# Moving the down-projection's weight rows to the split-weight slots, summing in place, and merging the operand stores

## The chip, the cores and the metric

The kernel runs on 1 core of one Trainium2 chip. The metric is the device time of one execution in microseconds (us); lower is better. The core's engines are PE (matrix products; PEld is its weight load), DVE (VectorE, elementwise work), ACT (ScalarE), POOL (GpSimd) and SP (SyncE, which here only issues DMAs). ACT issues DMAs too, from the same in-order instruction stream as its arithmetic.

## The reference, cut to what matters

One decoder block on 1024 tokens of width 1024: retention and sparse attention, merged, then a gated feed-forward part, all in float32. The change lies in the feed-forward part:

```
def conv_ffn(h, w_up, conv_w, conv_b, w_down):
    a, b = jnp.split(h @ w_up, 2, axis=-1)          # w_up: 1024 x 5632
    ac = conv_b + sum(conv_w[i] * a_pad[:, i:i + S] for i in range(CONV_W))
    return (jax.nn.gelu(ac) * b) @ w_down            # w_down: 2816 x 1024
```

## The kernel before, in words

**Products.** Every float32 product is made from three reduced-precision ones: each operand is split into a high and a low part (`split`, lines 129 and 130: ACT copies the high part, DVE subtracts it to get the low part) and `mm3` (lines 133 to 135) issues three matmuls of 128x128 by 128x512. Both feed-forward products are done as 2x2 block products with seven multiplications in place of eight (Winograd's form of Strassen's scheme), so that sums and differences of blocks of both operands have to be made first.

**Up-projection.** `up(f)` handles a pair of 128-column blocks of the hidden width (11 pairs). For each pair, `seven` (line 954) runs twice: once for the half `a` (which then goes through the convolution and GELU in `conv`, line 1002) and once for the half `b` (which multiplies the result, `out_b`, line 1012). Each run makes seven products of 12 matmuls. `up_weights` (line 903) loads two raw weight tiles `wu_raw` (line 908), forms the block sums `t12`, `t34` (lines 914, 915, 932, 933) and splits them: the sums into `wt`, the three plain blocks into `d11`, `d21`, `d22`. The seventh product of each run is put off into the next run (`late`), so `out_b(2)` of a pair (line 1016) runs inside the next pair.

**Operands of the down-projection.** When `out_b(2)` is done, lines 1026 to 1035 form four sums `s1` to `s4` of the gated result into two tiles `gs`, and ACT stores each to DRAM. Between the two runs of `seven`, `down_sums` (line 1037) loads two tiles of rows of `w_down` (`wd_raw`, line 1042), forms four sums into two tiles `ws` (lines 1048 to 1051), and ACT stores each (line 1053). With the three blocks of the gated result stored by line 1023 that is eleven stores per pair.

**Slots.** Tiles with one tag share a fixed number of slots. `wu_raw`, `wd_raw` and later `dn_raw` share three slots of 4 KB per partition (pool `wraw`, tag `raw`). `d11`, `d21`, `d22`, `gs` and `ws` share four slots with the tag `wh` and four with the tag `wl` (pool `wsp`). A load is issued when its slot is free. `rows` holds the gated result of a pair (`ac`) and is written again by the next pair's `conv`.

**Down-projection.** `down` (line 1092) runs over seven operands and 11 pieces each: `piece` (line 1069) loads a tile `dn_raw` with the row operand beside the weight operand, splits it, and 12 matmuls use it. Four of the seven operands come from the scratch `p_scr` (one DMA per piece), three from `g_scr` and `w_down` (two DMAs per piece).

**Order.** Each engine runs its own instructions in a fixed order. The order is chosen when the kernel is built, by a planner that lays the instructions on a simulated time line, takes what is ready, and prefers what stands earlier in the program. It is not written by hand here, and nothing reorders it on the chip: an engine that comes to an instruction whose data is missing waits there.

```
    wraw = ctx.enter_context(tc.tile_pool(name="wraw", bufs=3))
    wsp = ctx.enter_context(tc.tile_pool(name="wsp", bufs=4))
```

Of the kernel before, what the change touches and what calls it, by code (L numbers as in the profile page):

```python
# [10 lines left out]
F32 = mybir.dt.float32  # L11
# [7 lines left out]
P = 128  # L19
# [65 lines left out]
def tile_hybrid_block(ctx: ExitStack, tc: tile.TileContext, x, norm_mix, w_in, ret_gn_g,  # L85
# [4 lines left out]
    nc = tc.nc  # L90
    x, out = x[0], out[0]
# [5 lines left out]
    wraw = ctx.enter_context(tc.tile_pool(name="wraw", bufs=3))  # L97
    wsp = ctx.enter_context(tc.tile_pool(name="wsp", bufs=4))
# [8 lines left out]
    def scratch(name, n, shape):  # L107
        return [dram.tile(list(shape), F32, name=f"{name}{i}") for i in range(n)]
# [19 lines left out]
    def split(hi, lo, src):  # L128
        nc.scalar.activation(hi, src, AF.Copy)  # L129
        nc.vector.tensor_sub(lo, src, f32(hi))  # L130
# [9 lines left out]
    def weights(parts, kt=KD, raw_eng=None):  # L140

        n = sum(q[2] for q in parts)
        raw = wraw.tile([P, kt, n], F32, name="w_raw", tag="raw")
        c = 0
        for src, c0, w in parts:
            nc.sync.dma_start(raw[:, :, c:c + w],
                              src[:kt * P, c0:c0 + w].rearrange("(k p) c -> p k c", p=P))
            c += w
        wh = wsp.tile([P, kt, n], F32R, name="w_hi", tag="wh")
        wl = wsp.tile([P, kt, n], F32R, name="w_lo", tag="wl")  # L150
        split(wh, wl, raw)
        return wh, wl
# [413 lines left out]
    with ExitStack() as st:  # L566
# [32 lines left out]
        for h in range(H_R):  # L599
# [27 lines left out]
            if h < SPILL_Q:  # L627
                raw = wraw.tile([P, S], F32, name="q_raw", tag="raw")
# [28 lines left out]
            if h < SPILL_V:  # L657
                for hf in range(2):
                    raw = wraw.tile([P, 4, DV], F32, name="v_raw", tag="raw")
# [8 lines left out]
            for t in range(NT):  # L668
                hf, j = t // 4, t % 4
                c = slice(j * P, (j + 1) * P)  # L670
                tok = slice(t * P, (t + 1) * P)
                if wp:
                    ps = bank("mm")[:, 0:DV]
                    for k in range(KD):
                        wh, wl = wp[k // 4]
# [7 lines left out]
                if h == H_R - 1 and t == NT - 1:  # L683
# [4 lines left out]
                    for k in range(KD):  # L688
                        n = S if k < KD - 2 else 512
                        raw = wraw.tile([P, S], F32, name="r_raw", tag="raw")  # L690
# [78 lines left out]
    with ExitStack() as st:  # L769
        pool = st.enter_context(tc.tile_pool(name="mtmp", bufs=2))  # L770
        for mi in range(KD):
            wh, wl = weights([(w_ret_o, mi * P, P)])
# [40 lines left out]
    NP = NF // 2  # L813
    g_scr = {i: scratch(f"g_{i}", NP, (P, 512)) for i in ("a11", "a12", "s4")}

    p_scr = {i: scratch(f"p_{i}", NP, (P, 2, 512)) for i in ("s1", "s2", "s3", "a22")}

    def rms_row(t, xr, gain, dst=None):
        hx = fpool.tile([P, D], F32, name="hx", tag="ft", bufs=4)
# [15 lines left out]
    def block_pair(name):  # L835
        return [mpool.tile([P, 4, 512], F32R, name=name + i, tag="B") for i in "hl"]
# [3 lines left out]
    for ch in range(2):  # L840
        cs = slice(ch * 512, ch * 512 + 512)
        for t in (range(NT) if ch == 0 else (4, 5, 6, 7, 0, 1, 2, 3)):
            hf, j = t // 4, t % 4
# [11 lines left out]
            if t == 4:  # L855
                a22, s1 = block_pair("a22"), block_pair("s1")

                fa = big.tile([P, 2, 4, 512], F32, name="fa", tag="A")
            if t == 0:
                a11, a12 = block_pair("a11"), block_pair("a12")  # L860
                s4t = big.tile([P, 2, 4, 512], F32R, name="s4", tag="A")
                s4 = [s4t[:, i] for i in range(2)]
# [25 lines left out]
    s2, s3 = block_pair("s2"), block_pair("s3")  # L888
# [65 lines left out]
    def seven(c0, out):  # L954

        (t1, t2, t3, t4), (b11, b21, b22) = up_weights(c0)

        m = fpool.tile([P, 2, 512], F32, name="m", tag="ft", bufs=4)

        def kept(ps, i):  # L960
            nc.scalar.activation(m[:, i], ps, AF.Copy)
            return m[:, i]

        c = bank("sc")
        product(c, s1, t1, True, True)
        m5 = kept(c, 0)
        xb = bank("mm")
        product(xb, a11, b11, True, True)
        m1 = kept(xb, 1)
        while late:  # L970
            late.pop()()
        yb = bank("pt")
        product(yb, a12, b21, True, True)
        out(0, yb, m1)
        product(xb, s2, t2, False, True)
        u2 = kept(xb, 1)
        product(c, s4, b22, False, True)
        out(1, c, u2)
        product(xb, s3, t3, False, True)
        out(3, xb, m5)  # L980

        def last():
            product(xb, a22, t4, False, True)
            out(2, xb, None)
        late.append(last)

    def up(f):
        ar, ac = rows[:, 0], rows[:, 1]
        done = []

        def out_a(i, in0, in1):
            dst = ar[:, i % 2, T1 if i >= 2 else T0]
            if in1 is None:
                nc.scalar.activation(dst, in0, AF.Copy)
            else:
                nc.vector.tensor_add(dst, in0, in1)
            done.append(i)
            for e in range(2):
                if i in (e, e + 2) and e in done and e + 2 in done:
                    conv(e)  # L1000

        def conv(e):
            k = f + e
            nc.scalar.activation(ac[:, e], ar[:, e], AF.Identity, scale=cw[:, 2, k:k + 1],  # L1004
                                 bias=cw[:, 3, k:k + 1])
            nc.vector.scalar_tensor_tensor(ac[:, e, 1:S], ar[:, e, 0:S - 1], cw[:, 1, k:k + 1],
                                           ac[:, e, 1:S], op0=OP.mult, op1=OP.add)
            nc.vector.scalar_tensor_tensor(ac[:, e, 2:S], ar[:, e, 0:S - 2], cw[:, 0, k:k + 1],
                                           ac[:, e, 2:S], op0=OP.mult, op1=OP.add)
            nc.scalar.activation(ac[:, e], ac[:, e], AF.Gelu_apprx_tanh)  # L1010

        def out_b(i, in0, in1):
            tok = T1 if i >= 2 else T0
            g = ac[:, i % 2, tok]
            if in1 is None:
                nc.vector.tensor_mul(g, in0, g)
            else:
                nc.vector.tensor_add(in1, in0, in1)
                nc.vector.tensor_mul(g, in1, g)
            n = f // 2  # L1020
            if i != 2:
                dst = g_scr[("a11", "a12")[i]][n] if i < 2 else p_scr["a22"][n][:, 0, :]
                nc.scalar.dma_start(dst, g)
                return

            a11, a12, a21, a22 = (ac[:, e, t] for t in (T0, T1) for e in range(2))
            s = [wsp.tile([P, 2, 512], F32, name="gs", tag=t) for t in ("wh", "wl")]
            s1, s2, s3, s4 = (x[:, j] for x in s for j in range(2))
            nc.vector.tensor_add(s1, a21, a22)
            nc.vector.tensor_sub(s2, s1, a11)  # L1030
            nc.vector.tensor_sub(s3, a11, a21)
            nc.vector.tensor_sub(s4, a12, s2)  # L1032
            for name, v in (("s1", s1), ("s2", s2), ("s3", s3)):
                nc.scalar.dma_start(p_scr[name][n][:, 0, :], v)
            nc.scalar.dma_start(g_scr["s4"][n], s4)

        def down_sums():

            raws = []
            for e in range(2):  # L1040
                raw = wraw.tile([P, 2, 512], F32, name="wd_raw", tag="raw")
                nc.sync.dma_start(raw, w_down[(f + e) * P:(f + e + 1) * P, :].rearrange(
                    "p (h c) -> p h c", h=2))
                raws.append(raw)
            b11, b12, b21, b22 = (r[:, h] for r in raws for h in range(2))
            t = [wsp.tile([P, 2, 512], F32, name="ws", tag=t) for t in ("wh", "wl")]
            t1, t2, t3, t4 = (x[:, j] for x in t for j in range(2))
            nc.vector.tensor_sub(t1, b12, b11)
            nc.vector.tensor_sub(t2, b22, t1)
            nc.vector.tensor_sub(t3, b22, b12)  # L1050
            nc.vector.tensor_sub(t4, b21, t2)
            for name, v in (("s1", t1), ("s2", t2), ("s3", t3), ("a22", t4)):
                nc.scalar.dma_start(p_scr[name][f // 2][:, 1, :], v)

        seven(f * P, out_a)
        down_sums()
        seven(DFF + f * P, out_b)

    for f in range(0, NF, 2):
# [8 lines left out]

    def piece(name, n):
        raw = wraw.tile([P, 2, 512], F32, name="dn_raw", tag="raw")  # L1070
        if name in p_scr:
            nc.sync.dma_start(raw, p_scr[name][n])
        else:
            e, h = {"a11": (0, 0), "a12": (1, 0), "s4": (1, 1)}[name]
            r0 = (2 * n + e) * P
            nc.sync.dma_start(raw[:, 0], g_scr[name][n])
            nc.sync.dma_start(raw[:, 1], w_down[r0:r0 + P, h * 512:h * 512 + 512])
        w = mpool.tile([P, 2, 2, 512], F32R, name="dn", tag="B")
        split(w[:, 0], w[:, 1], raw)
        return w  # L1080
# [45 lines left out]
    for t in range(4):  # L1126
        final(t)

    ws = [piece("a22", n) for n in range(NP)]
    for j in range(4):  # L1130
        for n in range(NP):
            part(xb[j], ws[n], j, False, n == NP - 1, True)
        v = x1[4 + j][:, 0:512]
# [24 lines left out]
```

## Time and profile before

| | |
|---|---|
| median of 3 runs | 1798.89 us (1797.86 to 1800.18) |
| profiled execution | 1798.08 us |
| its span, first to last instruction | 1796.3 us |
| outside the span | 1.8 us |
| PE busy | 1722.9 us, 96% of the span |
| DVE busy | 1116.9 us, 62% |
| ACT busy | 802.2 us, 45% |
| mean granted PE clock | 0.987 |
| moved by DMA | 231.56 MB |

The busy share says how long an engine had something in work. PE's matmuls overlap in their pipeline, so that a busy PE need not be at its peak; the spacing of their starts says how fast they go. A wait names what came last for the waiting instruction. A timeline row begins with the start and the duration in us; a bracket at its end gives the idle time before it and what ended that.

### The profile page before, as it was taken

How to read it: one execution, taken by the hardware profiler on the slowest of the kernel's cores; microseconds unless marked ns; L12 is line 12 of the kernel's file. 1: busy time of each engine (PE TensorE's matmuls, PEld its weight loads, DVE VectorE, ACT ScalarE, POOL GpSimd, SP SyncE). 2: the span in 40 equal slices, each digit the busy share in tenths (PEclk: the TensorE clock that was granted, in tenths of full speed). 3: DMA queues.
4: the chain of work that ended last, by engine and by line, in shares of the span. 5: the costliest groups of instructions: out<-in, count | busy, mean ns of one | idle time of the engine just before them, and what ended most of it. 6: DMA issues, size and time to landing. Idle time of an engine off the chain costs nothing.

```text
span 1796.3 us, 24206 instructions
## 1 busy us (share of the span) xinstructions
PE 1722.9 (96%) x9005; PEld 1458.4 (81%) x9005; DVE 1116.9 (62%) x2332; ACT 802.2 (45%) x1425; POOL 86.6 (5%) x94
## 2 busy tenths in 40 slices
PE   7999999999999999999999896999998999999998
PEld 7888898988989998899777785877777777788886
DVE  6637676666766845565535348667667677665654
ACT  5435555455555744444544224433334343334442
POOL 1000000000000001221012000000000000000000
PEclk9999999999999999999999998999999999999999
DMA  6352222222221233222866311334444444487762
GB/s 207 106 144 75 64 67 63 63 74 74 62 71 57 74 118 98 83 86 78 257 216 216 133 71 69 114 135 153 154 150 157 142 143 139 158 296 241 232 209 107
DMA packets 177044, 231.56 MB, mean 129 GB/s; under 512 B 11558, under 2 KB 118558, under 8 KB 176926
## 3 DMA queue, kind: packets, MB, share of 16 engines
q1 hardware_dynamic: 137390, 167.34, 30.4%
q10 hardware_dynamic: 39536, 62.67, 9.4%
q8 instruction: 71, 1.16, 0.3%
q14 instruction: 47, 0.39, 0.1%
HBM read 163.12 MB, written 66.85 MB: 128 GB/s over the span
## 4 chain that ended last, share of the span: by engine, by line
PE 80%; DVE 8%; DMA 7%; ACT 2%; issue 2%; POOL 0%; SPq 0%; DVEq 0%; ACTq 0%; POOLq 0%
PE ps_mm L133 16%; PE ps_mm L134 15%; PE ps_mm L135 15%; PE ps_sc L135 4%; PE ps_sc L133 4%; PE ps_sc L134 4%; PE ps_pt L509 3%; PE ps_pt L135 2%; PE ps_pt L134 2%; PE ps_pt L133 2%; PE ps_sc L396 2%; PE ps_sc L395 2%; PE ps_pv L516 2%; PE ps_pv L515 2%; DMA sga<-ga_scr 1%
## 5 line engine op out<-in xcount | busy, mean ns | idle before, releaser
L133 PE MATMUL ps_mm<-hTh,w_hi 128*128 128x512 f32 x512 | 202.8, 396 | 3.1 <-DVE ql L130 2.5
L134 PE MATMUL ps_mm<-hTl,w_hi 128*128 128x512 f32 x512 | 202.4, 395 | 0.0
L135 PE MATMUL ps_mm<-hTh,w_lo 128*128 128x512 f32 x512 | 201.7, 394 | 0.0
L133 PE MATMUL ps_mm<-w_hi,hTh 128*128 128x256 f32 (+1 forms) x576 | 166.9, 290 | 2.5 <-ACT hTh L129 1.4
L135 PE MATMUL ps_mm<-w_hi,hTl 128*128 128x256 f32 (+1 forms) x576 | 167.2, 290 | 0.0
L134 PE MATMUL ps_mm<-w_lo,hTh 128*128 128x256 f32 (+1 forms) x576 | 166.7, 289 | 0.0
L130 DVE TENSOR_TENSOR w_lo<-w_raw,w_hi 128x1024 fp32r<-128x1024 f32 (+2 forms) x75 | 92.0, 1229 | 110.5 <-ACT w_hi L129 110.4
L130 DVE TENSOR_TENSOR dn<-dn_raw,dn 128x1024 fp32r<-128x1024 f32 x77 | 94.1, 1225 | 68.3 <-ACT dn L129 68.0
L129 ACT ACTIVATE dn<-dn_raw 128x1024 fp32r<-128x1024 f32 x77 | 81.6, 1061 | 105.6 <-DMA dn_raw<-in_w_down 38.3
L129 ACT ACTIVATE pth<-ps_pt 128x512 fp32r<-128x512 f32 x132 | 76.7, 593 | 107.1 <-PE ps_pt L509 106.2
L133 PEld LDWEIGHTS ps_mm<-hTh,w_hi 128*128 128x128 f32 x512 | 96.6, 189 | 22.8 <-DVE ql L130 2.9
L130 DVE TENSOR_TENSOR ptl<-ps_pt,pth 128x512 fp32r<-128x512 f32 x132 | 89.7, 688 | 39.1 <-ACT pth L129 38.8
L129 ACT ACTIVATE w_hi<-w_raw 128x1024 fp32r<-128x1024 f32 (+2 forms) x75 | 78.5, 1048 | 79.4 <-PE ps_mm L134 49.8
L133 PEld LDWEIGHTS ps_mm<-w_hi,hTh 128*128 128x128 f32 x576 | 110.4, 192 | 4.1 <-ACT hTh L129 1.8
L135 PEld LDWEIGHTS ps_mm<-hTh,w_lo 128*128 128x128 f32 x512 | 96.7, 189 | 19.0 <-DVE w_lo L130 0.3
L134 PEld LDWEIGHTS ps_mm<-hTl,w_hi 128*128 128x128 f32 x512 | 96.8, 189 | 18.3
L135 PEld LDWEIGHTS ps_mm<-w_hi,hTl 128*128 128x128 f32 x576 | 110.2, 191 | 1.2 <-DVE hTl L130 0.2
L134 PEld LDWEIGHTS ps_mm<-w_lo,hTh 128*128 128x128 f32 x576 | 110.4, 192 | 1.0
L1004 ACT ACTIVATE rows<-rows,cw 128x1024 f32<-128x1024 f32 x22 | 27.3, 1239 | 112.4 <-DVE gs L1032 111.0
L395 PE MATMUL ps_sc<-kst,q 128*128 128x512 f32 (+4 forms) x216 | 70.7, 333 | 0.0
L396 PE MATMUL ps_sc<-kst,q 128*128 128x512 f32 (+4 forms) x216 | 69.8, 329 | 0.0
L414 ACT ACTIVATE psl<-psl,nmax 128x1024 f32<-128x1024 f32 (+7 forms) x64 | 49.4, 772 | 21.6 <-DVE nmax L410 21.5
(371 smaller groups left out, 4472.5 us busy)
## 6 DMA issues: line engine op xcount, KB each, us to landing
w_raw<-in_w_in SPq DMA_DIRECT2D x48, 512.0 KB, 4.0
wu_raw<-in_w_up SPq DMA_DIRECT2D x44, 512.0 KB, 5.0
dn_raw<-p_s SPq DMA_DIRECT2D x33, 512.0 KB, 4.3
wd_raw<-in_w_down SPq DMA_DIRECT2D x22, 512.0 KB, 3.4
p_s<-ws ACTq DMA_DIRECT2D x33, 256.0 KB, 4.4
p_s<-gs ACTq DMA_DIRECT2D x33, 256.0 KB, 2.1
dn_raw<-in_w_down SPq DMA_DIRECT2D x33, 256.0 KB, 3.9
g_a<-rows ACTq DMA_DIRECT2D x22, 256.0 KB, 2.6
```

The lines of the kernel that those rows point to most:

```text
L129: nc.scalar.activation(hi, src, AF.Copy)
L130: nc.vector.tensor_sub(lo, src, f32(hi))
L133: nc.tensor.matmul(ps, ah, bh, start=start, stop=False, skip_group_check=more)
L134: nc.tensor.matmul(ps, ah, bl, start=False, stop=False, skip_group_check=more)
L135: return nc.tensor.matmul(ps, al, bh, start=False, stop=stop, skip_group_check=more)
L395: nc.tensor.matmul(dst, q1[:, r, :], kap, start=True, stop=False)
L396: nc.tensor.matmul(dst, q2[:, r, :], kap, start=False, stop=True)
L414: nc.scalar.activation(p_r, p_r, AF.Exp, bias=nmax[:, br, r:r + 1], scale=-1.0, accum_out=sums[:, br, r:r + 1])
L509: nc.tensor.transpose(pt[:, r, :], pr[r][:, kt * P:(kt + 1) * P], ident)
L515: nc.tensor.matmul(pv[0:DK], v[:, 0:DK], ptl, start=False, stop=False)
L516: nc.tensor.matmul(pv, v, pth, start=False, stop=last)
L1004: nc.scalar.activation(ac[:, e], ar[:, e], AF.Identity, scale=cw[:, 2, k:k + 1], bias=cw[:, 3, k:k + 1])
```

## The change

The two tiles of `w_down` rows are loaded into one `wh` and one `wl` slot in place of two `raw` slots, and their four sums are made in place, so that no `ws` tiles exist any more. Of the gated result's sums, `s1` and `s2` share one `wh` tile, while `s3` and `s4` overwrite two blocks of `ac` in `rows`. The four scratch arrays become one, `p_scr`, in which a partition's row holds two operands by four blocks of 512 numbers, ordered `s1`, `s3`, `a22`, `s2`. Through that order two neighbouring blocks of weights go out in one store each (two in place of four), and `s1` with `s2` in one store (a stride of three blocks). With the others that is eight stores per pair. `piece` now reads two runs of 2 KB per partition, 8 KB apart, where it read one run of 4 KB.

```diff
-    p_scr = {i: scratch(f"p_{i}", NP, (P, 2, 512)) for i in ("s1", "s2", "s3", "a22")}
+    p_scr = scratch("p_scr", NP, (P, 2, 4, 512))
+    p_at = {"s1": 0, "s3": 1, "a22": 2, "s2": 3}
...
             if i != 2:
-                dst = g_scr[("a11", "a12")[i]][n] if i < 2 else p_scr["a22"][n][:, 0, :]
+                dst = g_scr[("a11", "a12")[i]][n] if i < 2 else p_scr[n][:, 0, 2]
                 nc.scalar.dma_start(dst, g)
                 return
 
             a11, a12, a21, a22 = (ac[:, e, t] for t in (T0, T1) for e in range(2))
-            s = [wsp.tile([P, 2, 512], F32, name="gs", tag=t) for t in ("wh", "wl")]
-            s1, s2, s3, s4 = (x[:, j] for x in s for j in range(2))
+            st = wsp.tile([P, 2, 512], F32, name="gs", tag="wh")
+            s1, s2 = st[:, 0], st[:, 1]
             nc.vector.tensor_add(s1, a21, a22)
             nc.vector.tensor_sub(s2, s1, a11)
-            nc.vector.tensor_sub(s3, a11, a21)
-            nc.vector.tensor_sub(s4, a12, s2)
-            for name, v in (("s1", s1), ("s2", s2), ("s3", s3)):
-                nc.scalar.dma_start(p_scr[name][n][:, 0, :], v)
-            nc.scalar.dma_start(g_scr["s4"][n], s4)
+            nc.vector.tensor_sub(a21, a11, a21)
+            nc.vector.tensor_sub(a12, a12, s2)
+            nc.scalar.dma_start(p_scr[n][:, 0, 0:4:3], st)
+            nc.scalar.dma_start(p_scr[n][:, 0, 1], a21)
+            nc.scalar.dma_start(g_scr["s4"][n], a12)
 
         def down_sums():
 
             raws = []
             for e in range(2):
-                raw = wraw.tile([P, 2, 512], F32, name="wd_raw", tag="raw")
+                raw = wsp.tile([P, 2, 512], F32, name="wd_raw", tag=("wh", "wl")[e])
                 nc.sync.dma_start(raw, w_down[(f + e) * P:(f + e + 1) * P, :].rearrange(
                     "p (h c) -> p h c", h=2))
                 raws.append(raw)
             b11, b12, b21, b22 = (r[:, h] for r in raws for h in range(2))
-            t = [wsp.tile([P, 2, 512], F32, name="ws", tag=t) for t in ("wh", "wl")]
-            t1, t2, t3, t4 = (x[:, j] for x in t for j in range(2))
-            nc.vector.tensor_sub(t1, b12, b11)
-            nc.vector.tensor_sub(t2, b22, t1)
-            nc.vector.tensor_sub(t3, b22, b12)
-            nc.vector.tensor_sub(t4, b21, t2)
-            for name, v in (("s1", t1), ("s2", t2), ("s3", t3), ("a22", t4)):
-                nc.scalar.dma_start(p_scr[name][f // 2][:, 1, :], v)
+            nc.vector.tensor_sub(b11, b12, b11)
+            nc.vector.tensor_sub(b12, b22, b12)
+            nc.vector.tensor_sub(b22, b22, b11)
+            nc.vector.tensor_sub(b21, b21, b22)
+            for e in range(2):
+                nc.scalar.dma_start(p_scr[f // 2][:, 1, 2 * e:2 * e + 2], raws[e])
...
-        if name in p_scr:
-            nc.sync.dma_start(raw, p_scr[name][n])
+        if name in p_at:
+            nc.sync.dma_start(raw, p_scr[n][:, :, p_at[name]])
```

## Rows read from the trace of the kernel before

**Rows 1.** The page, parts 1 and 4: busy time by engine, and the chain by engine.
```profile
PE 1722.9 (96%) x9005; PEld 1458.4 (81%) x9005; DVE 1116.9 (62%) x2332; ACT 802.2 (45%) x1425; POOL 86.6 (5%) x94
...
PE 80%; DVE 8%; DMA 7%; ACT 2%; issue 2%; POOL 0%; SPq 0%; DVEq 0%; ACTq 0%; POOLq 0%
```

**Rows 2.** Windows by stage: stretch and length; PE, PEld, DVE, ACT, POOL; clock, DMA share, GB/s.
```profile
1160.00:1600.00 440.00, 413.43 (x1752) 330.20 (x1752) 304.72 (x409) 164.12 (x217) 0.00 (x0) 0.98 0.46 153
...
1620.00:1700.00 80.00, 80.00 (x355) 66.24 (x354) 48.69 (x45) 39.45 (x41) 0.00 (x0) 1.00 0.77 233
1700.00:1750.00 50.00, 50.00 (x223) 41.39 (x222) 28.49 (x29) 21.19 (x20) 0.00 (x0) 1.00 0.69 210
```

**Rows 3.** Windows from pair to pair (starts of line 1029): one pair, sum of eight.
```profile
1295.29:1338.55 43.26, 40.67 (x170) 32.37 (x169) 29.29 (x42) 15.48 (x21) 0.00 (x0) 0.96 0.41 140
...
sum 338.71, PE 317.62 PEld 253.31 DVE 233.84 ACT 123.65 POOL 0.00; mean PE 39.70 PEld 31.66 DVE 29.23 ACT 15.46 POOL 0.00
```

**Rows 4.** PE's timeline in that pair.
```profile
1291.62 0.39 PE L135 MATMUL ps_mm<-a22h,wt 128*128 128x512 f32 x1
...
1296.61 0.39 PE L135 MATMUL ps_mm<-s3h,wt 128*128 128x512 f32 x1
...
1297.06 0.39 PE L134 MATMUL ps_mm<-a11l,d 128*128 128x512 f32 x1
1298.44 0.50 PE L135 MATMUL ps_mm<-a11h,d 128*128 128x512 f32 x1 [0.99 <-DVE d L130]
...
1303.55 0.49 PE L133 MATMUL ps_pt<-a12h,d 128*128 128x512 f32 x1
...
1306.60 0.50 PE L135 MATMUL ps_pt<-a12h,d 128*128 128x512 f32 x1 [1.11 <-DVE d L130]
...
1310.58 0.39 PE L133 MATMUL ps_mm<-s2h,wt 128*128 128x512 f32 x1
```

**Rows 5.** PE's waits, 1160 to 1600 us: total us, times, longest us.
```profile
PE ps_pt L135 <- DVE d L130: 11.2, 10, 1.1
PE ps_mm L135 <- DVE d L130: 10.2, 10, 1.3
```

**Rows 6.** DVE's timeline in the same pair.
```profile
1294.09 0.69 DVE L1016 TENSOR_TENSOR rows<-ps_mm,rows 128x512 f32<-128x512 f32 x1 [6.52 <-PE ps_mm L135]
...
1297.10 0.68 DVE L1050 TENSOR_TENSOR ws<-wd_raw 128x512 f32<-128x512 f32 x1
1297.70 0.68 DVE L130 TENSOR_TENSOR d<-wu_raw,d 128x512 fp32r<-128x512 f32 x1
...
1302.85 0.69 DVE L915 TENSOR_TENSOR t<-wu_raw,t 128x512 f32<-128x512 f32 x1 [1.47 <-DMA wu_raw<-in_w_up]
```

**Rows 7.** SP's timeline in the same pair: its DMA issues, waits for slots included.
```profile
1297.81 6.77 SPq L908 DMA_DIRECT2D wu_raw<-in_w_up  x3
1309.51 5.71 SPq L1042 DMA_DIRECT2D wd_raw<-in_w_down  x2
1318.01 0.38 SPq L908 DMA_DIRECT2D wu_raw<-in_w_up  x1
```

**Rows 8.** DMA issues: KB each, median us from issue to landing.
```profile
wd_raw<-in_w_down SPq DMA_DIRECT2D x22, 512.0 KB, 3.4
...
p_s<-ws ACTq DMA_DIRECT2D x33, 256.0 KB, 4.4
p_s<-gs ACTq DMA_DIRECT2D x33, 256.0 KB, 2.1
...
g_s<-gs ACTq DMA_DIRECT2D x11, 256.0 KB, 4.7
```

**Rows 9.** ACT's timeline in the same pair.
```profile
1300.82 0.33 ACTq L1035 DMA_DIRECT2D g_s<-gs  x1
1301.19 1.24 ACT L1004 ACTIVATE rows<-rows,cw 128x1024 f32<-128x1024 f32 x1 [11.14 <-DVE gs L1032]
1302.85 0.64 ACT L129 ACTIVATE d<-wu_raw 128x512 fp32r<-128x512 f32 x1 [0.42 <-DMA wu_raw<-in_w_up]
```

## The prediction

> **What bounds the kernel now.** I read the shares of busy time and the chain first: PE is busy 96% of the span and holds 80% of the chain, DVE 8%, DMA 7% [rows 1]. So only PE's idle or slow stretches can be won. The windows by stage then say where they are. In the down-projection PE is busy 80.00 of 80.00 us and 50.00 of 50.00 us; in the up-projection 413.43 of 440.00 us, with DMA at 0.46 [rows 2]. The reader is to see that the change touches both stages and that only the up-projection has anything to give.
>
> Next, one period of the up-projection. Eight successive pairs take 338.71 us [rows 3], 42.34 us each. At full pace PE starts a matmul every 0.227 us: 22 steps from 1291.62 to 1296.61 [rows 4]. A pair has two runs of seven products of 12 matmuls, 168 matmuls, so 38.1 us at that pace. The loss is **4.24 us per pair**. PE's timeline shows it in two places. At the first, a step of 1.38 us (1297.06 to 1298.44) waits for the low part of a `d` tile; it costs 1.15 us over a normal step. At the second, from 1303.55 to 1310.58, PE starts 14 matmuls in 7.03 us where 3.18 would do: 3.85 us lost, to waits and, after them, to a granted clock that averages 0.96 over this pair [rows 3, 4]. Together 5.0 us in this pair, which is 0.9 us longer than the mean pair (43.26 against 42.34). Both stalls are in ten pairs: PE waited ten times for `d` on `ps_pt` and ten times on `ps_mm` [rows 5].
>
> Why is `d` late? DVE's timeline: after 6.52 us of idling for the late product, DVE runs line 1016 and then a solid burst. The first `d` low part, at 1297.70, stands behind two `gs` sums and two `ws` sums, the last of them line 1050 at 1297.10. Later in the burst DVE stands 1.47 us, up to 1302.85, for a `wu_raw` load, and the `b` half's sums and all that is split from them come behind that [rows 6]. SP's timeline says why the load is late: it is the first of three issued from 1297.81 on, just when line 1050 (1297.10 and 0.68 long) has read its `wd_raw` tile for the last time and its slot is free. Two `wd_raw` loads go out from 1309.51 on, once per pair, so that such a tile sits in one of the three `raw` slots for some 30 us, from there to the next pair's line 1050, while nothing uses it [rows 6, 7].
>
> **The change, part by part.**
>
> *`wd_raw` out of the `raw` slots.* Per pair the three slots then serve four tiles in place of six. At 1309.51 and up to 5.71 us later, when today two `wd_raw` loads take freed slots, the next pair's two `b` loads can go, and `wd_raw` no longer stands between [rows 7]. So the load that DVE waits for comes some 30 us before its use: DVE's 1.47 us and the second stall lose their cause. Taken as removed: 3.85 us in the pair shown, about 3.1 on the mean pair (4.24 less 1.15).
>
> *`ws` sums behind a later load.* A `wd_raw` tile now needs a `wh` and a `wl` slot, where `gs`, `d11`, `d21` and `d22` queue too. The four sums stay four at the spacing of 0.60 us, 2.4 us per pair, but cannot run before the new tile has landed, 3.4 us after its issue [rows 8]. If its slot comes with that of `gs`, the sums fall behind the `gs` sums and the first `d`, which then moves two places, 1.2 us, forward: 1298.38 becomes 1297.2, against the 1297.29 at which PE wants it. That takes the first stall of 1.15 us. DVE may stand idle for the new load as it does today for `wu_raw`; what is late next is then the low part of `wt` that the product `ps_sc` takes. Without stalls PE has four products of 2.7 us in hand from 1294.1 on (`s3`, `a11`, `a22`, `a12`), so that it wants `wt` at about 1305. DVE needs, from 1294.1, eight sums, results and `d` low parts of 0.6 us, four `ws` sums and a low part of `wt` of 1.2 us: 8.4 us, to 1302.5. So 2.5 us of waiting are covered. Bounds of this new wait: 0, and 3.1 us per pair if it gives back the whole second stall.
>
> *In-place `s3` and `s4`.* No DVE time changes. But `conv` of the next pair overwrites `ac`, so its first ACT instruction, at 1301.19 directly behind the last `gs` sum [rows 9], must now wait until the store of `s4` has landed: 2.1 us after issue by the nearest store rows, 4.7 by the row of this very store [rows 8]. The 4.7 were measured while three loads ran at once, which this change moves elsewhere; I take 2.1. Behind it on ACT stand the `d` and `wt` copies; with their loads in early they are ready before `conv` and can be placed ahead. Overwriting `a12` must wait for its store by line 1023 too; that one is issued before the late product's 6.52 us of DVE idling [rows 6], so it has landed: nothing.
>
> *Eight stores for eleven.* ACT issues three fewer per pair, at about 0.33 us each: 1 us of an engine that is busy 15.46 of 42.34 us [rows 3]. Nothing on the path. The bytes are the same.
>
> *Split reads in the down-projection.* Two runs of 2 KB in place of one of 4 KB. The stretch 1620 to 1700 reads mostly 4 KB runs at a share of 0.77 for 233 GB/s; 1700 to 1750 reads half of its pieces in 2 KB runs at 0.69 for 210 GB/s [rows 2]. Both are 0.0033 per GB/s, so the shorter runs cost nothing visible, and PE is at 100% over them. If that cover went, it would show as the first idle time of PE there.
>
> **The sum.** Both stalls gone would give 4.24 us in each of ten pairs, 42.4 us. For the new waits (`conv` on its store, the `w_down` sums on their load) I leave 1.0 us per pair, between 0 and 4.24, nearer to the low end because 2.5 us are covered on DVE. Gain 10 x 3.24 = 32.4 us. From the profiled execution of 1798.08 us that is 1765.7; the median of the runs lies 0.8 above it, so **1766.5 us**.
>
> A rule speaks on the `conv` wait. The row of the `s4` store says 4.7 us, the other `gs` stores 2.1 [rows 8]. The Trainium skill, "DMA: Bandwidth & Descriptors", section "Anatomy of one DMA — SWDGE (gpsimd) path", puts about 2.0 us of fixed cost, mostly the receipt of the write in memory, on a DMA, plus bytes over 436 GB/s; as an estimate from that page of the Trainium skill a 256 KB store takes 2.6 us. By it `conv` would begin at about 1303.4 and the sum would stay as it is; by the 4.7 us it would begin at 1305.5, and the slower rival below would have its condition. That page of the Trainium skill describes DMAs issued by GpSimd, and these are issued by ACT, so the rows decide.
>
> **Rivals.**
>
> *The wait is passed on, gain halved.* `wd_raw` gets its slot only with the `gs` tile, its load takes the 5.0 us that `wu_raw` takes today (1297.81 to 1302.85) [rows 6, 7], and DVE stands in the burst as before, with `wt` behind it. Then the second stall goes only by half: 10 x (1.15 + 1.55) = 27 less 1.0 per pair for `conv` gives 17, so 1782. For it: two tenants of `wh` and `wl` now stay through a load of 3.4 us and a store of 4.4 us, where `ws` stayed through the store alone [rows 8]. Against: 2.5 us of cover. Chance 0.17.
>
> *Slower: ACT is held by `conv`.* If the planner leaves `conv` ahead of the `d` and `wt` copies, as now, and the store of `s4`, issued at 1300.82 [rows 9], takes its 4.7 us, `conv` begins at 1305.5 in place of 1301.19, 4.3 us later, and the `d` copy goes from 1302.85 to 1307.2. With 0.6 us for the copy and 0.7 for the low part, PE resumes at 1308.5 and not at 1306.60: 1.9 us more per pair. The first stall lies ahead of `conv` and is still won, 1.15 us. Net 0.75 us more in ten pairs, 7.5 us: 1806. It makes the change slower from the landing at which the second stall grows by 1.15 us, about 3.9 us. For it: the 4.7. Against: the early loads let the copies go first, and the other stores land in 2.1. Chance 0.10.
>
> *It doesn't do what it says.* The order on DVE is fixed by a planner. If it leaves the sums and low parts of the `b` half where they are although the loads are early, the waits change their name and the time stays: 1796 to 1801. Chance 0.08, since the stall by name is a DMA that would be gone.
>
> **How the numbers follow.** Forecast 0.65, at 1755 to 1777. The range reaches from 1754 (all 42.4 us, and 2 us of the first pair's own start) to 1795, which takes in the passed-on wait and leaves out the slower rival and most of no change. A difference of 0.2%, 3.6 us, is about what a measurement of this kernel can tell from none. Faster 0.82 (forecast and passed-on wait), within 0.2% 0.07, slower 0.11.
>
> **What would show it.** Right: pairs 38.5 to 39.5 us apart at line 1029; no wait of DVE line 915 for `wu_raw`; PE's two waits for `d` gone or below 3 us each in total; SP's `wu_raw` loads of the `b` half issued about 30 us before line 915; down-projection still at 100% PE. Partly wrong: DVE waits for `wd_raw` at the first `ws` sum. Wrong: ACT's line 1004 waits for a store's landing with the `d` and `wt` copies behind it, or PE idle in the down-projection, or the granted clock staying low over more of the pair.

## The result and the profile after

The changed kernel takes 1754.83 us (median of 4 runs, 1752.51 to 1759.76) against 1798.38 us of the kernel before on the same chip: a ratio of 0.976 (95% interval 0.974 to 0.979), 43.6 us less. The profile below is of the longest of the four runs, 1759.76 us with a span of 1758.0; its counterpart is the 1798.08 us run on which the prediction worked. The mean granted PE clock rose from 0.987 to 0.992.

The page of the changed kernel, busy time and the chain by engine (against [rows 1]):

```profile
PE 1707.0 (97%) x9005; PEld 1455.2 (83%) x9005; DVE 1118.9 (64%) x2332; ACT 801.5 (46%) x1425; POOL 87.2 (5%) x94
...
PE 85%; DMA 7%; DVE 4%; ACT 2%; issue 1%; POOL 0%; SPq 0%; DVEq 0%; ACTq 0%; POOLq 0%
```

The counts are the same, DVE has 2 us more to do, and its share of the chain fell from 8 to 4%. Windows of the changed kernel (columns as in [rows 2]): ten periods of the up-projection from the first `gs` sum (now line 1030), its undisturbed middle, and a stretch of the down-projection:

```profile
1174.64:1561.80 387.16, 386.76 (x1702) 318.75 (x1701) 297.09 (x398) 162.42 (x214) 0.00 (x0) 1.00 0.51 174
1126.00:1560.00 434.00, 433.60 (x1901) 357.36 (x1902) 328.31 (x441) 180.49 (x239) 0.00 (x0) 1.00 0.49 168
1600.00:1710.00 110.00, 110.00 (x487) 91.10 (x486) 65.52 (x62) 49.33 (x51) 0.00 (x0) 1.00 0.70 218
```

Ten periods take 387.16 us, 38.7 each against 42.3 before [rows 3]; PE is busy 433.60 of 434.00 us at a granted clock of 1.00. The down-projection stays at 100% PE, and its DMA share per GB/s is 0.70/218 = 0.0032, against 0.0033 before [rows 2]. PE's waits from 1040 us to the end (total us, times, longest us), all that there are:

```profile
PE ps_pt L870 <- DVE hx L830: 10.7, 2, 5.5
PE ps_mm L135 <- DVE d L130: 2.7, 1, 2.7
PE ps_mm L133 <- ACT d L129: 0.6, 1, 0.6
PE ps_pt L133 <- ACT d L129: 0.3, 1, 0.3
```

Of the twenty waits of [rows 5] one is left, of 2.7 us, in the first pair; line 870 lies ahead of the up-projection. DVE's timeline around the late product of one pair, for comparison with [rows 6]:

```profile
1278.54 0.69 DVE L916 TENSOR_TENSOR t<-wu_raw,t 128x512 f32<-128x512 f32 x1
1279.26 0.69 DVE L934 TENSOR_TENSOR t<-wu_raw,t 128x512 f32<-128x512 f32 x1
...
1290.10 0.69 DVE L1017 TENSOR_TENSOR rows<-ps_mm,rows 128x512 f32<-128x512 f32 x1 [1.36 <-PE ps_mm L135]
1290.83 0.69 DVE L1030 TENSOR_TENSOR gs<-rows 128x512 f32<-128x512 f32 x1
1291.44 1.22 DVE L130 TENSOR_TENSOR wt<-t,wt 128x1024 fp32r<-128x1024 f32 x1
...
1294.91 0.68 DVE L130 TENSOR_TENSOR d<-wu_raw,d 128x512 fp32r<-128x512 f32 x1
...
1297.32 0.68 DVE L1047 TENSOR_TENSOR wd_raw<-wd_raw 128x512 f32<-128x512 f32 x1
```

The `b` half's sums (lines 916 and 934, before lines 915 and 933) now run 11 us ahead of the late product (line 1017, before 1016), where line 915 stood 8.8 us behind it. So the low part of `wt` follows the late product by 1.3 us, and the weight-row sums come last. ACT's timeline in the same pair:

```profile
1290.10 2.01 ACT L129 ACTIVATE wt<-t 128x1024 fp32r<-128x1024 f32 x2 [2.09 <-PE ps_mm L135]
1292.02 1.14 ACT L129 ACTIVATE d<-wu_raw 128x512 fp32r<-128x512 f32 x2
...
1297.43 0.33 ACTq L1036 DMA_DIRECT2D g_s<-rows  x1
...
1301.58 1.25 ACT L1005 ACTIVATE rows<-rows,cw 128x1024 f32<-128x1024 f32 x1 [2.27 <-DMA g_s<-rows]
```

ACT's waits at `conv` for that store and for the stores to `p_scr` in the changed kernel, 1130 to 1550 us:

```profile
ACT rows L1005 <- DMA g_s<-rows: 24.5, 8, 4.6
...
ACT rows L1005 <- DMA p_scr<-rows: 12.7, 5, 6.0
```

Two rows of its DMA issues, 1130 to 1560 us (columns as in [rows 8]):

```profile
g_a<-rows ACTq DMA_DIRECT2D x22, 256.0 KB, 2.1
...
g_s<-rows ACTq DMA_DIRECT2D x10, 256.0 KB, 5.4
```

`conv` (line 1005, before 1004) does wait for the store of `s4`, whose median landing is 5.4 us, but in this pair the `wt` and `d` copies stand ahead of it.

### The profile page after: what moved, and what is told of

It is laid out like the page before. It is cut to its first block, busy times and chain, and to the rows that moved or that the text cites. A ratio compares the mean times of both kernels' runs of the same rounds, so it can differ in the third digit from the quotient of the medians.

```text
span 1758.0 us, 24133 instructions
## 1 busy us (share of the span) xinstructions
PE 1707.0 (97%) x9005; PEld 1455.2 (83%) x9005; DVE 1118.9 (64%) x2332; ACT 801.5 (46%) x1425; POOL 87.2 (5%) x94
## 4 chain that ended last, share of the span: by engine, by line
PE 85%; DMA 7%; DVE 4%; ACT 2%; issue 1%; POOL 0%; SPq 0%; DVEq 0%; ACTq 0%; POOLq 0%
PE ps_mm L133 17%; PE ps_mm L135 17%; PE ps_mm L134 17%; PE ps_sc L135 5%; PE ps_sc L133 5%; PE ps_sc L134 5%; PE ps_pt L509 3%; DMA sga<-ga_scr 2%; PE ps_pt L135 2%; PE ps_pt L134 2%; PE ps_pt L133 2%; PE ps_sc L396 2%; PE ps_sc L395 2%; PE ps_pv L516 2%; PE ps_pv L515 2%
## 5 line engine op out<-in xcount | busy, mean ns | idle before, releaser
L135 PEld LDWEIGHTS ps_mm<-hTh,w_lo 128*128 128x128 f32 x512 | 96.3, 188 | 18.8 <-DVE w_lo L130 0.3
L134 PEld LDWEIGHTS ps_mm<-hTl,w_hi 128*128 128x128 f32 x512 | 96.3, 188 | 18.2
L129 ACT ACTIVATE wt<-t 128x1024 fp32r<-128x1024 f32 (+1 forms) x46 | 45.3, 1013 | 52.3 <-PE ps_mm L135 47.6
```

Source lines behind the costliest of these rows:

```text
L134: nc.tensor.matmul(ps, ah, bl, start=False, stop=False, skip_group_check=more)
L135: return nc.tensor.matmul(ps, al, bh, start=False, stop=stop, skip_group_check=more)
```

## The experiments

Twelve kernels were run, each beside the kernel before on the same chip. The order on every engine is chosen anew by the planner at each build, so that an edit acts through the order it leads to; where that order is the finding, its rows are shown. "PE busy" is of the 420 us from 1130 to 1550. The last two columns count from the late product, lowest to highest of ten pairs, in us: "load" is when the second `wu_raw` load of the `b` half is issued (a minus sign means ahead of the late product), "wt" is when the first low part of `wt` starts on DVE.

| kernel | median us (range) | ratio (95%) | PE busy | load | wt |
|---|---|---|---|---|---|
| the change | 1754.83 (1752.51–1759.76) | 0.976 (0.974–0.979) | 419.60 | -31.1 to -25.0 | 0.7 to 1.9 |
| 1 down half | 1759.16 (1758.63–1761.96) | 0.980 (0.978–0.983) | 416.32 | -29.7 to -21.8 | 1.9 to 2.4 |
| 2 gated half | 1762.72 (1760.77–1763.62) | 0.982 (0.979–0.985) | 415.69 | 2.0 | 10.2 to 10.9 |
| 3 in place in raw | 1754.99 (1754.26–1757.93) | 0.978 (0.975–0.980) | 420.00 | -18.2 to -15.7 | 1.9 to 2.4 |
| 4 move only | 1759.10 (1755.59–1762.43) | 0.980 (0.977–0.982) | 418.17 | -27.4 to -20.6 | 1.9 to 2.4 |
| 5 one call later | 1752.62 (1751.11–1755.60) | 0.975 (0.973–0.978) | 419.83 | -23.5 to -18.9 | 2.5 to 3.0 |
| 6 eleven stores | 1762.05 (1760.76–1763.85) | 0.980 (0.978–0.983) | 414.33 | -31.7 to -24.8 | 1.3 to 1.8 |
| 7 two raw slots | 1757.72 (1754.31–1759.44) | 0.978 (0.976–0.980) | 419.31 | -30.8 to -25.0 | 0.7 to 1.9 |
| 8 more stores | 1754.96 (1754.75–1755.50) | 0.977 (0.975–0.978) | 420.00 | -29.2 to -19.0 | 1.3 to 1.8 |
| 9 two tags | 1757.54 (1756.72–1760.40) | 0.978 (0.977–0.980) | 417.88 | -24.2 to -13.5 | 1.9 |
| 10 before + sums | 1797.59 (1792.36–1802.28) | 1.000 (0.999–1.002) | 394.46 | 7.6 to 8.2 | 16.3 to 18.8 |
| 11 gated half + sums | 1794.91 (1790.93–1798.37) | 0.998 (0.997–1.000) | 397.46 | 7.0 to 7.5 | 16.0 to 16.9 |
| 12 move only + sums | 1761.34 (1759.87–1764.94) | 0.981 (0.979–0.983) | 415.01 | -27.3 to -21.8 | 1.9 to 2.4 |

In the kernel before, PE busy is 396.39 of these 420 us, "load" is 3.3 to 3.7 and "wt" 12.0 to 12.9. In the pair of [rows 6], where line 1016 starts at 1294.09, its rows are

```profile
1305.86 0.68 DVE L130 TENSOR_TENSOR d<-wu_raw,d 128x512 fp32r<-128x512 f32 x1
1306.46 1.22 DVE L130 TENSOR_TENSOR wt<-t,wt 128x1024 fp32r<-128x1024 f32 x1
```

which is 12.4 us for `wt`. The column stands for the whole run of splits: the low part of `d` that PE waited for there, until 1306.60, comes right ahead of it.

**1. The down-projection's half alone.** Slots and in-place sums of `wd_raw`; four stores to the old scratch; the gated half as before.

```diff
-                raw = wraw.tile([P, 2, 512], F32, name="wd_raw", tag="raw")
+                raw = wsp.tile([P, 2, 512], F32, name="wd_raw", tag=("wh", "wl")[e])
...
-            nc.vector.tensor_sub(t1, b12, b11)
+            nc.vector.tensor_sub(b11, b12, b11)
```

> Only the weight rows' half: wd_raw in wh/wl slots with in-place sums, four separate stores, old scratch; the gated result's sums as before, eleven stores. Theory (the gain is the raw slots that wd_raw no longer holds until its sums run): the whole gain, 1753 to 1762 us, no wait of line 915 for wu_raw, and line 1004 still behind line 1032. Rival (the gain is the merged stores or the in-place sums of the gated result): 1795 to 1800. Rival (only the place of the first d low part on DVE counts): 1783 to 1790.

Measured: 1759.16 us. This half alone brings 0.020 of the 0.024.

**2. The gated half alone.** `s1` and `s2` in one `wh` tile, `s3` and `s4` over `rows`; eleven stores; `wd_raw` stays in `raw` and `ws` in `wh` and `wl`.

```diff
-            s = [wsp.tile([P, 2, 512], F32, name="gs", tag=t) for t in ("wh", "wl")]
+            st = wsp.tile([P, 2, 512], F32, name="gs", tag="wh")
...
-            nc.vector.tensor_sub(s3, a11, a21)
-            nc.vector.tensor_sub(s4, a12, s2)
+            nc.vector.tensor_sub(a21, a11, a21)
+            nc.vector.tensor_sub(a12, a12, s2)
```

> Only the gated result's half: s1 and s2 in one wh tile, s3 and s4 in place; eleven stores; wd_raw stays in raw slots with its sums in ws tiles. Theory: the raw slots are held as before, PE waits for d as before, 1790 to 1802 us; line 1004 now waits for the stores of s3 and s4. Rival (merged stores or in-place sums): a gain of 20 us or more. Rival (slower because conv waits for the stores): 1803 to 1815.

Measured: 1762.72 us. The theory missed: the half that moves no rows brings 0.018. DVE's timeline of this kernel in one pair:

```profile
1320.35 0.69 DVE L1016 TENSOR_TENSOR rows<-ps_mm,rows 128x512 f32<-128x512 f32 x1 [3.55 <-PE ps_mm L135]
1321.08 0.69 DVE L1029 TENSOR_TENSOR gs<-rows 128x512 f32<-128x512 f32 x1
1321.68 0.69 DVE L1048 TENSOR_TENSOR ws<-wd_raw 128x512 f32<-128x512 f32 x1
1322.29 0.68 DVE L130 TENSOR_TENSOR d<-wu_raw,d 128x512 fp32r<-128x512 f32 x1
...
1327.33 0.69 DVE L915 TENSOR_TENSOR t<-wu_raw,t 128x512 f32<-128x512 f32 x1 [0.75 <-DMA wu_raw<-in_w_up]
...
1330.94 1.22 DVE L130 TENSOR_TENSOR wt<-t,wt 128x1024 fp32r<-128x1024 f32 x1
```

Its DVE's wait over 1130 to 1550 us:

```profile
DVE t L915 <- DMA wu_raw<-in_w_up: 8.6, 10, 1.0
```

The wait behind the rows is still there ten times, 8.6 us in all, and the order is much like that of before, though line 1050 has gone ahead of the late product. Two sums are ahead of the first `d`, not four and a result of line 996 (1.94 us after line 1016 against 3.61), and line 915 comes after 6.98 us and not 8.76. With all of this 1.7 to 1.8 us earlier, nearly all of the stall is gone.

**3. In place, rows left in `raw`.** The four sums overwrite `wd_raw` where it is, no `ws` tiles (`tensor_sub(b11, b12, b11)` and so on, in the `raw` slots).

> wd_raw stays in the raw slots, but its sums are made in place, so that they need no ws tile and wait for no wh or wl slot. Theory, in the form that the hold lasted because the sums stood in line for ws tiles behind gs: the rows leave the raw slots after load, sums and store, some 10 to 15 us, and most of the gain is there, 1753 to 1768 us. Rival (six tiles per pair are too many for three slots whatever the hold): 1790 to 1800. In this rival line 915 still waits for wu_raw ten times.

Measured: 1754.99 us, as good as the change. DVE's wait for `wu_raw` over 1130 to 1550 us in this kernel:

```profile
DVE t L932 <- DMA wu_raw<-in_w_up: 15.9, 12, 2.0
```

PE is busy all 420 us while DVE still waits 15.9 us for `wu_raw`. In the kernel before, DVE's wait over the same stretch is

```profile
DVE t L915 <- DMA wu_raw<-in_w_up: 17.3, 10, 3.3
```

So the wait by name is nearly the same in size; what changed is that it lies ahead of the late product (line 932, by some 13 us in the pair near 1282), where PE has work in hand.

**4. The move alone.** Only the tag of `wd_raw` as in run 1; the `ws` tiles and all else as before.

> Only the tag of wd_raw is changed: rows in wh/wl slots, sums still in ws tiles, all eleven stores. Theory: raw slots are free, 1753 to 1765 us; the two more tenants of wh and wl per pair may cost up to 5 us through late d tiles. Rival (in place is needed, since rows and ws together crowd wh and wl): 1775 or more, with PE waiting for d.

Measured: 1759.10 us. Moving the tile is by itself enough too.

**5. One call later.** The kernel before, with the weight-row sums asked for after the second run of products:

```diff
-        down_sums()
         seven(DFF + f * P, out_b)
+        down_sums()
```

> The kernel before with one edit of order: down_sums is called after the second run of seven in place of between the two, so that the weight rows are loaded into raw slots behind the b half's two wu_raw tiles. No slot, sum or store is changed. Theory (the b half's second wu_raw waits for a slot that wd_raw holds): that wait goes, 1753 to 1770 us, though the rows may now hold up the next a half. Rival (relief of the three slots, or of the stores, is needed): 1790 to 1800.

Measured: 1752.62 us, the lowest median of all, though its range overlaps that of the change. DVE's timeline of this kernel in one pair:

```profile
1278.17 0.69 DVE L1016 TENSOR_TENSOR rows<-ps_mm,rows 128x512 f32<-128x512 f32 x1 [1.96 <-PE ps_mm L135]
...
1280.11 0.69 DVE L1048 TENSOR_TENSOR ws<-wd_raw 128x512 f32<-128x512 f32 x1
1280.71 1.22 DVE L130 TENSOR_TENSOR wt<-t,wt 128x1024 fp32r<-128x1024 f32 x1
```

Its DVE's waits for loads over 1130 to 1550 us:

```profile
DVE ws L1049 <- DMA wd_raw<-in_w_down: 12.8, 10, 2.9
DVE t L915 <- DMA wu_raw<-in_w_up: 11.5, 9, 2.2
DVE t L914 <- DMA wu_raw<-in_w_up: 4.7, 8, 0.9
```

DVE waits 29 us for loads in these 420 us, more than in the kernel before, and PE loses 0.17 us: the `wt` low part comes first, the waiting behind it.

**6. Eleven stores.** The changed kernel with the old scratch layout and separate stores; tags and in-place sums kept.

> The changed kernel without merged stores: old scratch layout, eleven stores, reads of 4 KB runs; moved rows and all in-place sums stay. Theory: the same as the changed kernel, 1751 to 1759 us, since ACT's issue time is off the path. Rival (merged stores carry part of the gain): 1765 or more.

Measured: 1762.05 us, between the two expectations; 7 us over the change by the medians, with intervals that just touch. One pair holds half of what PE loses. ACT's and DVE's timelines there:

```profile
1216.66 1.45 ACTq L1034 DMA_DIRECT2D p_s<-rows  x1
1222.88 1.25 ACT L1004 ACTIVATE rows<-rows,cw 128x1024 f32<-128x1024 f32 x1 [6.47 <-DMA p_s<-rows]
```

```profile
1224.16 1.28 DVE L1006 SCALAR_TENSOR_TENSOR rows<-rows,cw 128x1023 f32<-128x1023 f32 x1 [3.99 <-ACT rows L1004]
...
1234.35 1.22 DVE L130 TENSOR_TENSOR wt<-t,wt 128x1024 fp32r<-128x1024 f32 x1
```

PE's timeline behind it, in the same kernel:

```profile
1235.63 0.79 PE L135 MATMUL ps_sc<-s1h,wt 128*128 128x512 f32 x1 [2.89 <-DVE wt L130]
```

Here `conv` stands ahead of the `wt` copies and waits 6.47 us for a store. DVE stands 3.99 us for the result of `conv`, is busy without a gap from there on, and makes the low part of `wt` at the end of that burst, and PE stands 2.89 us for it. So `conv` did hold up PE once, as in the slower rival, but by way of DVE and not through late copies alone. Three waits of up to 0.9 us for a `wt` copy come on top (2.8 us in all). Whether the merging itself or the other order of this build costs the 7 us stays open.

**7. Two raw slots.** The changed kernel with one more tile in the `raw` slots. It was meant to hold one of the three through the up-projection: its last use stands behind the up-projection in the program.

```diff
+    held = wraw.tile([P, 2, 512], F32, name="held", tag="raw")
+    nc.sync.dma_start(held, w_down[0:P, :].rearrange("p (h c) -> p h c", h=2))
...
     for f in range(0, NF, 2):
         up(f)
...
+    nc.vector.tensor_copy(held[:, 0, 0:1], held[:, 0, 1:2])
```

> The changed kernel with one of the three raw slots held by an idle tile from the start of the up-projection to its end, so that four wu_raw tiles per pair go through two slots. Theory: loads are late again, part or all of the gain is given back, 1765 to 1800 us, and DVE waits for wu_raw. Rival (three raw slots are more than needed once the rows are out): 1753 to 1760.

Measured: 1757.72 us. The run does not test what it was meant to. The planner put the tile's last use right behind its load, ahead of the up-projection:

```profile
1024.78 0.15 DVE L1065 COPY held<-held 128x1 f32<-128x1 f32 x1 [3.43 <-DMA held<-in_w_down]
```

From there on all three slots were free, and the run repeats the change. Whether two slots would serve is not shown.

**8. More stores.** The changed kernel, `s4` stored three more times, to scratch that nothing reads.

```diff
             nc.scalar.dma_start(g_scr["s4"][n], a12)
+            for again in again_scr:
+                nc.scalar.dma_start(again[n], a12)
```

> The changed kernel with the store of s4 issued three more times to other scratch, so that conv's first ACT instruction waits longer (three more issues of 0.33 us and their landing). Theory (the wait of conv for the stores is covered): 1751 to 1760 us although ACT's line 1005 waits 30 to 60 us in total. Rival (conv's wait is just at the edge of PE's cover): 1765 or more, with PE waiting for ACT.

Measured: 1754.96 us. The wait of `conv` (line 1006 here) on ACT over 1130 to 1550 us:

```profile
ACT rows L1006 <- DMA again<-rows: 18.1, 9, 4.2
```

PE is busy all 420 us and does not feel `conv`'s wait. But the extra stores did not lengthen it: with 5.4 us for stores to `p_scr` it is 23.5 us, where the changed kernel has 37.2 (24.5 and 12.7). So the run shows cover only for waits of the size seen, up to 4.2 us, and not for longer ones.

**9. Two tags.** The kernel before; both `gs` tiles in `wh`, both `ws` tiles in `wl`.

```diff
-name="gs", tag=t) for t in ("wh", "wl")]
+name="gs", tag=t) for t in ("wh", "wh")]
...
-name="ws", tag=t) for t in ("wh", "wl")]
+name="ws", tag=t) for t in ("wl", "wl")]
```

> The kernel before with only two tags changed: both gs tiles in wh, both ws tiles in wl; wd_raw stays in raw, no in-place sum, eleven stores. Theory after the first eight runs (in the kernel before a chain runs from line 1016 through gs, the ws sums that stand behind it for wh and wl slots, the release of a raw slot, the wu_raw load and line 915 to PE; whatever takes a link out of it gives the whole gain): the ws sums need not follow gs any more, the chain is cut, 1751 to 1761 us. Rival (rows must leave the raw slots or sums be in place): 1785 to 1800.

Measured: 1757.54 us. With no tile moved to or from `raw` and no sum in place, the stall goes once the `ws` tiles no longer share slots with the `gs` tiles. The `ws` sums then run behind their own load: in the pair whose line 1016 starts at 1288.83, the first row tile's load is issued at 1294.35 and line 1050, its last reader, ends at 1306.2. That is 12 us in the slot, where the prediction read some 30.

**10 to 12. Redundant sums.** In the kernel before, in run 2's and in run 4's, the first weight-row sum is made four times, which adds 3 x 0.60 = 1.8 us of DVE per pair.

```diff
             nc.vector.tensor_sub(t1, b12, b11)
+            nc.vector.tensor_sub(t1, b12, b11)
+            nc.vector.tensor_sub(t1, b12, b11)
+            nc.vector.tensor_sub(t1, b12, b11)
```

> The kernel before with the sum t1 made four times in place of once (three more DVE instructions per pair at a spacing of 0.6 us, 1.8 us, on the ws sums that the raw slot's release waits for). Theory (chain sets the pair): 1.5 to 2.5 us more per pair, 1812 to 1823 us. Rival (PE's loss comes from something else and DVE has room): 1795 to 1802.

> The gated result's half alone (as in the second run of this study) with the sum t1 made four times. Theory (that half only shortens the chain by about 2 us and leaves it just short of PE's need): 1.8 us put back bring the stalls back, 1772 to 1800 us, PE waiting for d again. Rival (that half cuts the chain): 1759 to 1766.

> Only the tag of wd_raw changed (as in the fourth run) with the sum t1 made four times. Theory (with the rows out of raw the sums are on no chain to PE): no change against that run, 1755 to 1764 us. Rival (the gain there is also only a matter of 2 us on DVE): 1772 or more.

Measured: 1797.59 us for the kernel before with them, no change, where the theory wanted 14 to 25 us more; 1794.91 for the gated half, 32.2 us more than without (0.017 by the ratios); 1761.34 for the move, 2.2 us more with overlapping ranges. PE's waits over 1130 to 1550 us in the gated half with the sums:

```profile
PE ps_pt L133 <- ACT d L129: 16.3, 12, 4.1
PE ps_sc L133 <- ACT wt L129: 3.5, 3, 1.2
PE ps_pt L135 <- DVE d L130: 2.7, 5, 0.5
```

DVE's timeline of that kernel in one pair:

```profile
1295.99 0.69 DVE L1016 TENSOR_TENSOR rows<-ps_mm,rows 128x512 f32<-128x512 f32 x1 [5.92 <-PE ps_mm L135]
...
1308.13 0.69 DVE L915 TENSOR_TENSOR t<-wu_raw,t 128x512 f32<-128x512 f32 x1 [1.62 <-DMA wu_raw<-in_w_up]
...
1312.34 1.22 DVE L130 TENSOR_TENSOR wt<-t,wt 128x1024 fp32r<-128x1024 f32 x1
```

Line 915 is 12.1 us behind line 1016 (7.0 without the sums): 5.1 us more for 1.8 us of added work, since the order changed too and a part of `conv` now stands ahead of it. PE waits for the copies of `d`. In the move with the sums, `wt` still follows line 1016 by 2.4 us, and at most little is lost. So the gated half alone sits near an edge, and the moved rows leave slack for 1.8 us per pair. Why the kernel before does not get worse is open: it too has line 915 12.2 us behind line 1016 (8.8 without). PE's waits on `ps_mm`, the first stall, fall from 9.3 us in nine to 2.3 in two, those on `ps_pt`, the second, grow from 10.5 to 22.1 us, and the total stays.

## Why the prediction was right

The forecast was 1766.5 us, the range 1754 to 1795. The 1754.83 measured lies 0.8 us inside its fast end, and just outside the 1755 to 1777 for which the chance of 0.65 stood. The profiled executions differ by 38.3 us, although the changed kernel's was 3.8 us behind when the up-projection began: its first matmul on `a11` starts at 1113.81 us against 1110.03. From there to the last matmul of the down-projection it takes 636.7 us against 678.7: 42.0 us less, nearly the 42.4 that the prediction had as the whole loss of ten pairs.

*What bounds the kernel, and the loss of 4.24 us per pair.* Right. The gain is PE's, in the up-projection alone, and the down-projection is as it was. The loss was more than waits, though. Windows of the kernel before over the second stall of [rows 4]:

```profile
1303.50:1307.00 3.50, 1.90 (x7) 0.96 (x7) 3.50 (x6) 3.36 (x5) 0.00 (x0) 1.00 1.00 350
1307.00:1310.60 3.60, 3.60 (x11) 2.77 (x10) 3.60 (x5) 3.03 (x5) 0.00 (x0) 0.53 0.32 102
1310.60:1320.00 9.40, 9.40 (x43) 7.76 (x42) 9.16 (x14) 4.75 (x7) 0.00 (x0) 1.00 0.38 121
```

After a stretch in which PE is busy 1.90 of 3.50 us, the granted clock is 0.53, near the lower level of 1.2 GHz, and steps take 0.43 us in place of 0.227; seven of them cost 1.4 us of this stall's 3.85. All of it comes back with the waits: 1.00 over the changed kernel's up-projection.

*"`wd_raw` out of the `raw` slots".* The gain that it names came, with most of its signs: DVE's sums of the `b` half run ahead of the late product, and line 916 (before, 915) no longer waits for `wu_raw`. The loads of the `b` half go out 14 to 18 us ahead of its sums, against 4 to 7 before, and not the 30 that the prediction named. The trace of the kernel before bears out its link between the rows and the late load. SP's wait there, 1130 to 1550 us:

```profile
SPq L908 <- DVE ws L1050: 160.2, 9, 19.4
```

The same wait in run 9:

```profile
SPq L908 <- DVE ws L1050: 47.6, 10, 6.7
```

But the length of DVE's wait for `wu_raw` is not what cost PE: it is 17.3 us before, 15.9 in run 3 and 16.2 in run 5 (11.5 and 4.7), where PE loses next to nothing. Nor is the move needed: runs 3, 5 and 9 leave the rows in `raw` and gain as much. Whether fewer slots would do is not shown, since run 7 left them free. The change and all faster runs but run 2 share one thing in all ten pairs: the `b` half's second load goes out 13 us or more ahead of the late product and the splits start within 3.0 us behind that product (table). In the kernel before that load comes 3.3 us or more behind the late product, and the splits 12.0 us or more. By the prediction's own working PE wants `wt` some 11 us behind the late product (1305 against 1294.1), and run 2, with 10.2 to 10.9, comes just in time.

So the chain in the kernel before reads: `ws` sums behind `gs` sums (run 9 parts them), the rows' slot freed only by the `ws` sums (runs 1, 3 and 4), the load behind the rows (run 5), and the `b` half's sums and splits last, with PE waiting. Each of these five single edits brings 37 to 44 us (0.020 to 0.025 of some 1798). The step is right on the gain and too narrow on the cause: it named one link of a chain of which any link would do. Two things are not shown. That the `ws` sums stand where they do for want of a slot follows from the shared tags and run 9, not from a row. And how much of the loss is a wait on the chip and how much the order that the planner built around it, no run separates. The kernel before was late by little: 1.7 to 1.8 us earlier is enough in run 2, and run 11 puts 32 us back. How late the load is does not give the loss by itself: in run 10 it is 4 us later than in the kernel before, and the time is the same.

*"`ws` sums behind a later load".* Right: in the pair shown, the weight-row sums come 7.2 us after the late product, behind the splits, and PE waits for `d` once, in the first pair.

*"In-place `s3` and `s4`".* The price was wrong, the effect right. I took 2.1 us for the landing of the `s4` store, and it is 5.4. ACT waits 24.5 us for it, and 12.7 us, up to 6.0 at a time, for stores to `p_scr`, which the prediction did not price. The condition that the slower rival put on the landing, 3.9 us, was met; its other condition, `conv` ahead of copies, was met in some pairs, and PE lost time by it in one, 0.30 us (the last of its waits above). Run 6 shows `conv` hold up PE once for longer, 2.89 us, by way of DVE. The estimate of 2.6 us for such a store that the prediction gave from the Trainium skill, "DMA: Bandwidth & Descriptors", section "Anatomy of one DMA — SWDGE (gpsimd) path", is within half a microsecond of the 2.1 of the `g_a` stores and less than half of these 5.4.

*"Eight stores for eleven" and "split reads".* The reads cost nothing, as predicted. For the stores, nothing on the path was predicted; run 6 bounds their worth at 7 us without settling it.

*The sum.* The mis-sized term is the 1.0 us per pair left for new waits: PE is not busy for 0.40 us in the 434 us shown, so it was near 0. That is 10 of the 11.7 us between forecast and result. The bound of all 42.4 us was the better value: the new waits lay behind the splits that PE wanted sooner.

*The rivals.* The wait was not passed on (no DVE wait for the rows costs PE), and the change does what it says. DVE's order was changed by the planner, as the forecast needed.

## What to carry to other kernels

A wait named in the profile is worth what it delays: compare where PE's next operand stands on the waiting engine. DVE's waits for `wu_raw` of 17.3 us went with 23.6 us of idle PE in the kernel before, and 15.9 us of them with none in run 3. Where a loss repeats with every period, follow the chain of slots from one period to the next and try the cheapest edit to any link: here one moved call gave as much as the whole change. Run the halves of a change apart, and put a little redundant work back into the better ones: a half that gains nearly everything may lose it again for 2 us of work. And look in the trace whether an edit does what it is for: the copy that was to hold a slot in run 7 ran at once.

## What was unexpected

- Stores of one size landed after very different times: 256 KB took 2.1 us (`g_a`) and 5.4 us (`s4`) in the changed kernel, and ACT stood idle 6.47 us before `conv` for a store of `s3` in run 6. Why is not shown.
- The same 1.8 us of DVE per pair cost 32.2 us of time in run 11 (2.9 us per pair over eleven pairs), 2.2 us within overlapping ranges in run 12, and nothing in run 10.
- A wait of 2.89 us in run 6 was followed by a granted clock of 0.65 over 4.4 us, with steps of up to 0.43 us; the waits of under 1 us in run 1 left the mean clock at 1.00.
